# End of attention: the gate's operands of the first token block made in weight buffers at steps 116 to 119, and later loads moved behind the output weights

## The chip, the cores and the metric

The kernel runs on one NeuronCore of one Trainium2 chip. The metric is the time of one execution on the device in microseconds (us), median of several runs. Engine names are those of the profile: PE is TensorE, DVE is VectorE, ACT is ScalarE, POOL is GpSimd, SP is SyncE, the queue from which most DMA transfers are issued.

## What is computed

One layer of a hybrid encoder: a state-space branch and a chunked attention branch share one input projection; their outputs are normalised, concatenated and projected, and a SwiGLU feed-forward part follows. Sizes: 2048 tokens, model width 1024, 512 channels for each branch, 8 attention heads of 64, chunks of 64 frames with 8 chunks to the left, feed-forward width 2816, float32.

```python
def reference(x, ...):
    h = rmsnorm(x, norm_mix_g[l])
    proj = h @ w_in[l]
    y_ssm = s5_mixer(u_ssm, ...)            # ends: y = gelu(y); y = y * sigmoid(y @ w_glu + b_glu)
    y_att = chunked_attention(q, k, v, attn_rel_bias[l])
    mixed = concatenate([rmsnorm(y_ssm, norm_ssm_out_g[l]), rmsnorm(y_att, norm_att_out_g[l])])
    x = x + mixed @ w_out[l]
    h = rmsnorm(x, norm_ffn_g[l])
    x = x + (silu(h @ w_gate[l]) * (h @ w_up[l])) @ w_down[l]
    return rmsnorm(x, norm_final_g)
```

## The kernel before

Matmuls of high precision are made of three: an operand is split into a high half (a cast on ACT) and a low half (a subtraction on DVE); `split` (line 177) does this, and `mm3` (line 171) adds hi*hi, hi*lo and lo*hi in PSUM. Profile lines 81 and 84 are the wrappers through which all matmuls and transposes go.

**Attention** (`att_phase`, line 733) runs over 128 steps: 4 token blocks of 512, 4 head pairs, 2 heads, 4 query pieces. A step's scores `sc` come from PE; DVE adds the bias and finds the maximum (line 937), ACT takes the exponential (line 940), PE transposes (`pt`), and the transposed piece is split into `pth` (ACT, line 956) and `ptl` (DVE, line 957). After four pieces the products with `v` go to `pj`; `ya` (lines 981 and 990) is the attention output, which is stored to `ya_s` (line 991). Between these, generators called units bring in other work piece by piece: projections of later token blocks (their weights lie in three buffers `w` of [128, 2, 1024], line 753, last used for the last projections), the state-space branch, and from step 120 (`GSTART`) on the first `MIX_N` pieces of `mix_phase`.

Two helpers set the order: `behind()` (line 739) makes an instruction stand behind the last exponential in its engine's list (`k.least`), and `issue_after(k.low)` behind the last `ptl`. The lists are fixed when the program is built; each engine works its list in order, and SP's DMAs stand in one list too.

A pool `lp` lasts beyond attention and keeps the tags listed in `LASTING` (line 39), among them the split gate weights `Wg`, which are made at steps 90 to 102, and `raw`, two buffers of [128, 1024] that from step 107 hold the four tiles `ys` of block 0. The state-space output of blocks 0 and 1 is fetched at steps 107 to 110 (`y0`), goes through gelu on ACT at steps 109 to 117, and is copied into `ys` on POOL (line 1058).

**The mixing phase** (`mix_phase`, line 1088) takes the four token blocks in turn. For each block `take` provides `ys`, `load` splits the four tiles of `ys` into `gh0..3` and `gl0..3` of the phase's own pool `my`, and `glu` makes the gate: four groups f of 12 matmuls of 128x512 (four k-tiles by three), then sigmoid and multiply. For block 0 the gate is in attention's spare PSUM tiles `pf`, the biases are added on DVE into `yr` (line 1183), and one sigmoid and four multiplies (lines 1185, 1187) follow at the end. For block 1 the groups go to tiles `big`. `rstd1` sums squares over channels (`pf<-ones,sq`, a few narrow matmuls) and takes the reciprocal roots on DVE (`newton`, lines 110 to 118, the last of which is `k.last_root`), `spread` puts them over all partitions with four transposes, and `rstd2` (line 1204) multiplies `ya` or `ys` by them. `mixed` splits the results into `m0..m7`, and `w_out` multiplies by the split output weights `woh`, `wol`, adds to `xt` and stores. `split_wo` splits eight pieces of w_out: two loaded early into buffers `xt` of pool `wr`, four into tiles `m..` of pool `mx`, two more into the `xt` buffers again once these are split.

`fetch` (line 1131) loads `yr`, the raw state-space output of blocks 2 and 3, with four DMAs; it is called when block 2 is taken. Between blocks 1 and 3 `pre_steps` prepares the first feed-forward inputs in spare tiles that `pre_tiles` hands out. The seam, where PE goes from w_out to the feed-forward part, is at about 911 us.

At the end of attention the code is:

```python
b, nxt = take(0), take(1)
for f in range(4):
    with tc.issue_after(k.least):
        load(b, f)
    yield
...
for f in range(4):
    load(nxt, f)
yield
pb = bk()
spread(k, te, pb[:, :512], b.o[0], 0)
rstd2(b, 0, pb[:, :512])
for n, _ in enumerate(glu(nxt, bk)):
```

`bank()` gives a tile of attention's PSUM pool; `bk()` gives one of that pool or, once attention has handed PSUM over, a `big` tile of two banks.

Of the kernel before, what the change touches and what calls it, by code (L numbers as in the profile page):

```python
# [16 lines left out]
P = 128  # L17
# [20 lines left out]
GATES = 90, 94, 98, 102  # L38
LASTING = "hi0", "lo0", "hi1", "lo1", "hi2", "lo2", "xt", "raw"
R1 = 10  # L40
# [692 lines left out]
def att_phase(k, ident, S, aw, x0, roots):  # L733

    tc, nc, io, pfs = k.tc, k.nc, k.io, k.pfs
    with ExitStack() as cx:
# [303 lines left out]
        for s in range(N + LAG + 2):  # L1040
# [9 lines left out]
            for o in TURNED.get(s % 32, ORDER) if s < N - 32 else ORDER:  # L1050
# [12 lines left out]
                elif o == "f":  # L1063
# [9 lines left out]
                    if s in GATES:  # L1073
                        q = GATES.index(s)
                        tags = [("xt", XB)] * 2 if q == 3 else [(f"hi{q}", 1), (f"lo{q}", 1)]
                        k.Wg[q] = [k.t(k.lp, n, [P, DS], F32R, bufs=c) for n, c in tags]
                        with behind():
                            split(k, k.Wg[q][0][:], k.Wg[q][1][:], wg[q // 2][:, q % 2 * DS : q % 2 * DS + DS])
            if s in FETCHES:
                f = FETCHES.index(s)  # L1080
                nc.sync.dma_start(k.y0[:, f], S["y"][:, f * P : (f + 1) * P, :128].rearrange("j p t -> p j t"))
        yield mix


MIX_N = 21


def mix_phase(k, S, bank):
# [3 lines left out]
    with ExitStack() as cx:  # L1092
# [10 lines left out]
        def load_wo(n, pool, tag, **kw):  # L1103
            raw = k.t(pool, tag, [P, 1024], **kw)
            nc.sync.dma_start(raw[:], io["w_out"][QS[n] * P : (QS[n] + 1) * P, :])
            return raw

        def split_wo(raws):
            for n, q in enumerate(QS):
                W[q] = k.t(mx, f"woh{q}", [P, D], F32R), k.t(mx, f"wol{q}", [P, D], F32R)  # L1110
                raw = raws[n] if n < len(raws) else load_wo(n, wr, "xt")
                with tc.issue_after(k.last_root) if n > 1 else nullcontext():
                    split(k, W[q][0][:], W[q][1][:], raw[:])
# [17 lines left out]
        def fetch(sb):  # L1131
            yrs[0] = k.t(my, "yr", [P, 4, L, 128])
            for f in range(4):
                nc.sync.dma_start(yrs[0][:, f], S["y"][:, f * P : (f + 1) * P, sb * 64 : sb * 64 + 128].rearrange("j p t -> p j t"))  # L1134

        def take(sb):
# [6 lines left out]
            else:  # L1143
                yt = k.t(my, "ys", [P, 4, SB])
                b.ys = [yt[:, f] for f in range(4)]
            b.g = []
            if sb == 2:
# [21 lines left out]
        def glu(b, bank, late=False):  # L1169
# [5 lines left out]
            for f in range(4):  # L1175
                ps = bank()
                cs = slice(f * P, (f + 1) * P)
                for q in range(4):
                    mm3(te, ps[:, :512], Wg[q][0][:, cs], Wg[q][1][:, cs], b.g[q][0][:], b.g[q][1][:], q == 0, q == 3)
                    if q < 3:  # L1180
                        yield
# [77 lines left out]
        def pre_tiles():  # L1259
            while True:  # L1260
                for f in range(4):
                    for m in "hl":
                        yield k.t(my, f"g{m}{f}", [P, SB])
                t = k.t(my, "yr", [P, 4, L, 128])[:].rearrange("p a b c -> p (a b c)")
                for i in range(8):
                    yield t[:, i * SB : (i + 1) * SB]

        yrs[0] = k.t(my, "yr", [P, 4, L, 128])
        b, nxt = take(0), take(1)
        for f in range(4):  # L1270
            with tc.issue_after(k.least):
                load(b, f)
            yield
        g = glu(b, bank, True)
# [12 lines left out]
        for f in range(4):  # L1287
            load(nxt, f)
        yield

# [600 lines left out]
```

## Time and profile before

| | |
|---|---|
| median of 3 runs | 2211.99 us |
| lowest, highest | 2210.46, 2216.73 us |
| profiled execution, its own time | 2214.67 us |
| profiled execution, span | 2212.9 us |
| PE busy | 2155.7 us, 97% |
| DVE, ACT busy | 69%, 46% |
| mean granted clock of PE | 0.992 |

The span is measured by the profiler from the first to the last instruction. PE is busy nearly throughout, so the places that matter are those where it stands still or runs at a lower granted clock. The places of the change lie between 597 us (the first copy into `ys`) and 715 us; attention's last transposed piece is split at 674 us, and the first w_out matmul of block 0 starts at 693.73 us. A row of the timeline gives start, duration, engine, line, operation, output<-inputs (buffer numbers left out), shape, count, and in brackets the idle time before it and what ended it.

### The profile page before, as it was taken

To read this page: it belongs to the slowest core of one execution; us is meant where nothing else is said; L and a number is where in the kernel's file an instruction comes from. 1 tells how busy PE (TensorE), PEld (TensorE's weight loads), DVE (VectorE), ACT (ScalarE), POOL (GpSimd) and SP (SyncE) were. 2 spreads that over 40 slices of the span, in tenths; PEclk is the share of its full clock that TensorE was granted. 3 is DMA by queue.
4 is the path that set the end of the run, shared out by engine and by line. 5 is a ranking of instruction groups with operands and counts; after the bars stand their busy time and mean duration, and the time that the engine had idled before them with its cause. 6 is when DMAs were issued, how large, how long until landed. Compare 5 with 4: busy or idle time off the path is not lost.

```text
span 2212.9 us, 30057 instructions
## 1 busy us (share of the span) xinstructions
PE 2155.7 (97%) x10606; PEld 1816.1 (82%) x10606; DVE 1534.3 (69%) x2667; ACT 1008.1 (46%) x1684; POOL 371.5 (17%) x839
## 2 busy tenths in 40 slices
PE   8999999999998999999999999999999999999998
PEld 6787898998977888788888887888888788888887
DVE  8767566565568657767776768767665477689785
ACT  6356566555677521533333345333333443354332
POOL 3367777676110000000000000000000100000000
PEclk9999999999999999999999999999999999999999
DMA  9788977665633346835555657545332395465552
GB/s 323 240 284 268 303 229 241 210 202 174 202 111 138 119 143 218 262 100 182 177 174 190 211 189 262 194 159 203 110 113 102 123 390 179 164 220 197 193 216 77
DMA packets 194423, 431.20 MB, mean 195 GB/s; under 512 B 19744, under 2 KB 37200, under 8 KB 187168
## 3 DMA queue, kind: packets, MB, share of 16 engines
q1 hardware_dynamic: 186448, 404.05, 54.7%
q0 software_dynamic: 7824, 25.24, 3.8%
q8 instruction: 83, 1.36, 0.3%
q14 instruction: 68, 0.56, 0.1%
HBM read 290.00 MB, written 131.10 MB: 190 GB/s over the span
## 4 chain that ended last, share of the span: by engine, by line
PE 61%; DMA 5%; DVE 2%; ACT 1%; issue 1%; SPq 0%; DVEq 0%; ACTq 0%
PE X L81 21%; PE ps L81 17%; PE Y L81 11%; PE big L81 6%; PE W L81 5%; DMA acc<-x 2%; DMA lo<-hc 1%; DMA x<-xt 1%; DVE xt L1239 0%; DMA hd<-wc 0%; DMA m<-in_w_out 0%; ACT hi L179 0%; DMA hc<-gh 0%; DVE acc L1664 0%; SPq L1134 0%
## 5 line engine op out<-in xcount | busy, mean ns | idle before, releaser
L81 PE MATMUL X<-hi,c 128*128 128x512 f32 x1408 | 451.7, 392 | 9.6 <-DVE c L179 5.0
L81 PE MATMUL ps<-hd,hd 128*128 128x512 f32 (+1 forms) x1920 | 428.8, 384 | 3.4 <-DVE hd L179 2.0
L81 PEld LDWEIGHTS ps<-hd,hd 128*128 128x128 f32 x1920 | 353.3, 188 | 75.1 <-DVE hd L179 2.7
L81 PEld LDWEIGHTS X<-hi,c 128*128 128x128 f32 x1408 | 265.8, 189 | 66.5 <-DVE c L179 5.9
L81 PE MATMUL X<-lo,c 128*128 128x512 f32 x704 | 275.3, 391 | 0.0
L179 ACT CAST hd<-hd 128x1536 fp32r<-128x1536 f32 (+1 forms) x106 | 147.5, 1394 | 230.7 <-DMA hd<-hq 164.9
L81 PE MATMUL Y<-hi,c 128*128 128x512 f32 x704 | 224.8, 390 | 1.5 <-DVE u L1526 1.5
L179 DVE TENSOR_TENSOR hd<-hd 128x1536 fp32r<-128x1536 f32 (+1 forms) x106 | 174.2, 1645 | 35.9 <-ACT hd L179 35.1
L179 DVE TENSOR_TENSOR c<-S,c 128x512 fp32r<-128x512 f32 x176 | 120.9, 688 | 101.0 <-ACT c L179 100.8
L1630 POOL DMA_DIRECT2D hd<-hq x7 | 5.2, 745 | 1072.0 <-PE X L81 1060.7
L1522 ACT COPY u<-X 128x512 f32<-128x512 f32 x132 | 77.4, 587 | 197.7 <-PE X L81 197.7
L179 ACT CAST c<-S 128x512 fp32r<-128x512 f32 x176 | 109.4, 622 | 121.7 <-PE Y L81 62.0
L81 PE MATMUL big<-m,woh 128*128 128x512 f32 x512 | 161.2, 396 | 0.0
L81 PEld LDWEIGHTS Y<-hi,c 128*128 128x128 f32 x704 | 132.7, 189 | 29.9 <-DVE u L1526 2.2
L1664 DVE TENSOR_TENSOR acc<-acc,ps 128x512 f32<-128x512 f32 x196 | 130.3, 683 | 38.5 <-PE ps L81 38.0
L81 PEld LDWEIGHTS X<-lo,c 128*128 128x128 f32 x704 | 132.9, 189 | 27.5
L179 ACT CAST c<-raw 128x512 fp32r<-128x512 f32 x132 | 82.2, 623 | 148.8 <-PE Y L81 73.0
L81 PE MATMUL pf<-hi,w 128*128 128x512 f32 x416 | 148.8, 410 | 0.0
L81 PE MATMUL Y<-lo,c 128*128 128x512 f32 x352 | 137.2, 390 | 0.0
L957 DVE TENSOR_TENSOR ptl<-pt,pth 128x640 fp32r<-128x640 f32 (+3 forms) x152 | 98.3, 646 | 46.1 <-ACT pth L956 42.1
L940 ACT ACTIVATE s<-s,mn 128x640 f32<-128x640 f32 (+4 forms) x128 | 97.9, 765 | 51.4 <-DVE mn L937 50.9
L956 ACT CAST pth<-pt 128x640 fp32r<-128x640 f32 (+3 forms) x152 | 83.8, 551 | 81.2 <-PE pt L84 75.7
(494 smaller groups left out, 4281.3 us busy)
## 6 DMA issues: line engine op xcount, KB each, us to landing
w<-wss SPq DMA_DIRECT2D x36, 1024.0 KB, 6.1
hq<-g SPq DMA_DIRECT2D x140, 256.0 KB, 2.1
hd<-hq SPq DMA_DIRECT2D x35, 768.0 KB, 4.4
hd<-wc SPq DMA_DIRECT2D x35, 768.0 KB, 5.9
raw<-in_w_gate SPq DMA_DIRECT2D x44, 512.0 KB, 3.6
raw<-in_w_up SPq DMA_DIRECT2D x44, 512.0 KB, 4.1
wc<-px SPq DMA_DIRECT2D x66, 256.0 KB, 3.1
wss<-w SPq DMA_DIRECT2D x12, 1024.0 KB, 6.3
```

Source lines behind the costliest of these rows:

```text
L81: return self.tc.keep_in_program_order(self.tc.nc.tensor.matmul(*a, **b))
L179: return nc.scalar.copy(hi, raw), nc.vector.tensor_tensor(lo, raw, f32(hi), op=ALU.subtract)
L940: nc.scalar.activation(s[:, :nk], s[:, :nk], AF.Exp, bias=mn[:], scale=-1.0, accum_out=sums[sb, pr][:, hh, qp : qp + 1])
L956: nc.scalar.copy(pth[:, a:b, qp, :], pt[:, a:b, :])
L957: k.low = nc.vector.tensor_tensor(ptl[:, a:b, qp, :], pt[:, a:b, :], f32(pth[:, a:b, qp, :]), op=ALU.subtract).ins
L1522: nc.scalar.copy(u[:], ps[:])
L1630: (nc.gpsimd if aside else nc.sync).dma_start(f32(lo), src.rearrange("g p c -> p g c"))
L1664: V.tensor_tensor(a, a, ps[:], op=ALU.add)
```

## The change

- The tag `w` joins `LASTING`, so that the three weight buffers are kept until the feed-forward part.
- At step 116 two of them become `k.G`; at steps 116 to 119 (`HEADS`) one tile of block 0's `ys` each is split into a quarter of `k.G`, under `behind()`. The four pieces that did this in `mix_phase` go, and `MIX_N` is 17 instead of 21.
- All four blocks use `k.G` as gate operands (`gate_operand`); `gh*` and `gl*` go. `ys` of blocks 1 and 3 lies in the third `w` buffer. `pre_tiles` hands out pieces of `w` buffers in place of the `g` tiles.
- The `yr` loads are put behind the last load of w_out.
- Only splits of w_out from the fifth on stand behind the last reciprocal root, instead of from the third on.
- The `spread` of block 0's attention roots and the multiplies `rstd2` are written one piece earlier, with a tile of `bank()`.

```diff
-LASTING = "hi0", "lo0", "hi1", "lo1", "hi2", "lo2", "xt", "raw"
+LASTING = "hi0", "lo0", "hi1", "lo1", "hi2", "lo2", "xt", "raw", "w"
+HEADS = 116, 117, 118, 119
...
+            if s == HEADS[0]:
+                k.G = [k.t(k.lp, "w", [P, 2, 1024], F32R, bufs=WB) for _ in range(2)]
+            if s in HEADS:
+                f = HEADS.index(s)
+                with behind():
+                    split(k, *gate_operand(k, f), k.ys[f])
...
-MIX_N = 21
+MIX_N = 17
+def gate_operand(k, f):
+    fs = slice(f % 2 * SB, f % 2 * SB + SB)
+    return k.G[f // 2][:, 0, fs], k.G[f // 2][:, 1, fs]
...
-            nc.sync.dma_start(raw[:], io["w_out"][QS[n] * P : (QS[n] + 1) * P, :])
+            k.last_wo = nc.sync.dma_start(raw[:], io["w_out"][QS[n] * P : (QS[n] + 1) * P, :]).ins
...
-                with tc.issue_after(k.last_root) if n > 1 else nullcontext():
+                with tc.issue_after(k.last_root) if n > 3 else nullcontext():
...
-                nc.sync.dma_start(yrs[0][:, f], S["y"][...])
+                with tc.issue_after(k.last_wo):
+                    nc.sync.dma_start(yrs[0][:, f], S["y"][...])
...
-                yt = k.t(my, "ys", [P, 4, SB])
-                b.ys = [yt[:, f] for f in range(4)]
-            b.g = []
+                if sb == 1:
+                    k.y1 = k.t(k.lp, "w", [P, 4, SB], bufs=WB)
+                b.ys = [k.y1[:, f] for f in range(4)]
...
-            gh, gl = k.t(my, f"gh{f}", [P, SB], F32R), k.t(my, f"gl{f}", [P, SB], F32R)
-            split(k, gh[:], gl[:], b.ys[f])
-            b.g.append((gh, gl))
+            split(k, *gate_operand(k, f), b.ys[f])
...
-                for f in range(4):
-                    for m in "hl":
-                        yield k.t(my, f"g{m}{f}", [P, SB])
+                for _ in range(2):
+                    t = k.t(k.lp, "w", [P, 4, SB], bufs=WB)
+                    for i in range(4):
+                        yield t[:, i]
...
         b, nxt = take(0), take(1)
-        for f in range(4):
-            with tc.issue_after(k.least):
-                load(b, f)
-            yield
         g = glu(b, bank, True)
...
         for f in range(4):
             load(nxt, f)
+        pb = bank()
+        spread(k, te, pb, b.o[0], 0)
+        rstd2(b, 0, pb[:])
         yield
...
-        pb = bk()
-        spread(k, te, pb[:, :512], b.o[0], 0)
-        rstd2(b, 0, pb[:, :512])
```

Three places show what this does to the lists. The first is DVE in the last attention steps, before and now; `s,mn` is the bias and maximum of a step, `k` the last keys, `gl` and `w` the low halves of the gate's operands, made from `raw`.

```order
L857 TENSOR_TENSOR k_1693_7796<-pf_7852,k_1693_7796 64x512
L857 TENSOR_TENSOR k_1696_7799<-pf_7852,k_1696_7799 64x512
L179 TENSOR_TENSOR gl_1726_7979<-raw_7422,gh_1725_7978 128x512
L957 TENSOR_TENSOR ptl_7920<-pt_7952,pth_7919 128x5x128
L937 ISA s_7987,mn_7988<-sc_7982,nba_98 128x640
L937 ISA mn_7988 128x1
L967 RECIPROCAL rs_8044<-sm_7635 128x8
L957 TENSOR_TENSOR ptl_7920<-pt_7992,pth_7919 128x5x128
L179 TENSOR_TENSOR gl_1733_8001<-raw_7422,gh_1732_8000 128x512
L179 TENSOR_TENSOR gl_1735_8005<-raw_7423,gh_1734_8004 128x512
```

Now:

```order
L180 TENSOR_TENSOR w_7856<-raw_7422,w_7856 128x512
L958 TENSOR_TENSOR ptl_7745<-pt_7827,pth_7744 128x5x128
L938 ISA s_7867,mn_7868<-sc_7862,nbb_1553 128x640
L938 ISA mn_7868 128x1
L856 SCALAR_TENSOR_TENSOR q2l_7795<-pf_7802,q2h_7794 64x512
L856 SCALAR_TENSOR_TENSOR q2l_7798<-pf_7802,q2h_7797 64x512
L180 TENSOR_TENSOR w_7856<-raw_7422,w_7856 128x512
L958 TENSOR_TENSOR ptl_7745<-pt_7871,pth_7744 128x5x128
L938 ISA s_7900,mn_7901<-sc_7895,nbb_1553 128x640
L938 ISA mn_7901 128x1
L180 TENSOR_TENSOR w_7857<-raw_7423,w_7857 128x512
```

The first three subtractions now stand beside the last queries `q2l`, ahead of the last keys (`k`), and the fourth a few rows further on; before, all four stood behind the keys; the casts on ACT move in the same way.

The second is DVE from the last subtraction of block 1's operands to the `ya` multiplies (line 1204 before, 1216 now), before and now. `pf_8332` is a tile in attention's PSUM bank 1, `big_8392` one of the tiles after the hand-over.

```order
L179 TENSOR_TENSOR gl_1810_8343<-ys_7973,gh_1809_8342 128x512
L1187 TENSOR_TENSOR raw_7422<-raw_7422,yr_7972 128x512 x2
L1187 TENSOR_TENSOR raw_7423<-raw_7423,yr_7972 128x512 x2
L1123 TENSOR_TENSOR sq_8319<-sq_8319,sg_8321 128x512
L981 TENSOR_TENSOR ya_8203<-pj_8350,yt_8367 64x512
L1123 TENSOR_TENSOR sq_8319<-sq_8319,sg_8324 128x512
L990 TENSOR_TENSOR ya_8203<-ya_8203,pj_8370 128x512
L1123 TENSOR_TENSOR sq_8319<-sq_8319,sg_8327 128x512
L1204 SCALAR_TENSOR_TENSOR ya_1758_8115<-ya_1758_8115,ga_7967,big_8392 128x512
L1204 SCALAR_TENSOR_TENSOR ya_1759_8116<-ya_1759_8116,ga_7967,big_8392 128x512
```

Now:

```order
L180 TENSOR_TENSOR w_7857<-w_7981,w_7857 128x512 x2
L1216 SCALAR_TENSOR_TENSOR ya_1737_8042<-ya_1737_8042,ga_7975,pf_8332 128x512
L1199 TENSOR_TENSOR raw_7422<-raw_7422,yr_7980 128x512 x2
L1199 TENSOR_TENSOR raw_7423<-raw_7423,yr_7980 128x512 x2
L1136 TENSOR_TENSOR sq_8313<-sq_8313,sg_8315 128x512
L1216 SCALAR_TENSOR_TENSOR ya_1738_8043<-ya_1738_8043,ga_7975,pf_8332 128x512
L1136 TENSOR_TENSOR sq_8313<-sq_8313,sg_8318 128x512
L1216 SCALAR_TENSOR_TENSOR ya_1739_8044<-ya_1739_8044,ga_7975,pf_8332 128x512
L1136 TENSOR_TENSOR sq_8313<-sq_8313,sg_8321 128x512
L1216 SCALAR_TENSOR_TENSOR ya_1740_8045<-ya_1740_8045,ga_7975,pf_8332 128x512
L982 TENSOR_TENSOR ya_8226<-pj_8345,yt_8362 64x512
L991 TENSOR_TENSOR ya_8226<-ya_8226,pj_8365 128x512
```

The four multiplies moved ahead of the last two `ya` of attention and between the adds of squares. On PE the first gate group of block 1, `big_8387`, takes banks 0 and 1, and its first matmul waits for the last of these four multiplies; before, `big_8392` had banks 0 and 1, the first two groups had banks 6 and 7 and 4 and 5, and it was the second that waited, for line 990.

The third is SP's list behind the store of attention's next to last `ya_s`, before and now.

```order
L1134 DMA yr_8908<-y_65 128x8x128 x4
L1105 DMA m_1834_8499<-in_w_out 128x1024
L1105 DMA m_1835_8501<-in_w_out 128x1024
L1105 DMA m_1836_8503<-in_w_out 128x1024
L1105 DMA m_1837_8505<-in_w_out 128x1024
L1105 DMA xt_8545<-in_w_out 128x1024
L1105 DMA xt_8551<-in_w_out 128x1024
L1166 DMA ya_1911_8933<-ya_s_66 128x512
```

Now:

```order
L1118 DMA m_1820_8485<-in_w_out 128x1024
L1118 DMA m_1821_8487<-in_w_out 128x1024
L1118 DMA m_1822_8489<-in_w_out 128x1024
L1118 DMA m_1823_8491<-in_w_out 128x1024
L1118 DMA xt_8531<-in_w_out 128x1024
L1118 DMA xt_8537<-in_w_out 128x1024
L1148 DMA yr_8894<-y_65 128x8x128 x4
L1178 DMA ya_1889_8911<-ya_s_66 128x512
```

The four `yr` loads moved from ahead of the six loads of w_out to behind them.

More of the change, by code (lines that the diff above doesn't have):

```diff
@@ L1133, in fetch @@
             for f in range(4):
-                nc.sync.dma_start(yrs[0][:, f], S["y"][:, f * P : (f + 1) * P, sb * 64 : sb * 64 + 128].rearrange("j p t -> p j t"))
+                with tc.issue_after(k.last_wo):
+                    nc.sync.dma_start(yrs[0][:, f], S["y"][:, f * P : (f + 1) * P, sb * 64 : sb * 64 + 128].rearrange("j p t -> p j t"))
         def take(sb):
@@ L1178, in glu @@
                 for q in range(4):
-                    mm3(te, ps[:, :512], Wg[q][0][:, cs], Wg[q][1][:, cs], b.g[q][0][:], b.g[q][1][:], q == 0, q == 3)
+                    mm3(te, ps[:, :512], Wg[q][0][:, cs], Wg[q][1][:, cs], *gate_operand(k, q), q == 0, q == 3)
                     if q < 3:
```

## The prediction

> **What bounds the kernel now.** The first view read was the chain of waits over the whole program. TensorE holds most of it, so a stall anywhere else counts only where TensorE stands still for it.
>
> ```profile
> PE 61%; DMA 5%; DVE 2%; ACT 1%; issue 1%; SPq 0%; DVEq 0%; ACTq 0%
> ```
>
> The second view was the timeline of TensorE (start, duration, what, and in brackets its idle time before and the releaser), from the last attention steps to the output projection. Its idle places there, two rows without idle that mark where block 1's gate and w_out begin (677.76, 693.73), and the end of the mixing phase:
>
> ```profile
> 640.04 1.33 PE L84 MATMUL pt<-ident,s 128*128 128x128 f32 x5 [1.89 <-DVE ptl L957]
> 643.01 1.33 PE L84 MATMUL pt<-ident,s 128*128 128x128 f32 x5 [0.57 <-DVE ptl L957]
> 674.57 0.50 PE L81 MATMUL pj<-ptl,v 128*128 128x512 f32 x1 [0.36 <-DVE ptl L957]
> 677.76 0.48 PE L81 MATMUL big<-gh,hi 128*128 128x512 f32 x1
> 682.89 0.47 PE L81 MATMUL big<-gh,hi 128*128 128x512 f32 x1 [2.14 <-DVE ya L990]
> 693.73 0.62 PE L81 MATMUL big<-m,woh 128*128 128x512 f32 x2
> 698.49 0.50 PE L81 MATMUL big<-m,wol 128*128 128x512 f32 x1 [2.78 <-DVE wol L179]
> 699.62 0.50 PE L81 MATMUL big<-m,wol 128*128 128x512 f32 x1 [0.17 <-DVE wol L179]
> 914.64 0.47 PE L81 MATMUL X<-hi,c 128*128 128x512 f32 x1 [3.26 <-DVE xt L1239]
> 916.99 1.22 PE L81 MATMUL X<-hi,c 128*128 128x512 f32 x2 [1.64 <-DVE c L179]
> ```
>
> The last two rows are the seam, where the feed-forward part (X) follows the last output projection. The stalls at 698.49 and 699.62 hang on the split output weights. The third view, the chain of waits inside this stretch, says why those weights are late: SP, which issues the loads, issued the four yr loads (line 1134) late, and the loads of w_out (line 1105) only behind them.
>
> ```profile
> 680.25 0.37 SPq L1134
> 686.75 6.97 DMA m<-in_w_out
> 697.30 2.28 DVE wol L179 x2
> 699.62 8.69 PE big L81 x37
> ```
>
> The fourth view is the table by stage, columns: the stretch, its length, busy time and instructions of TensorE, its weight loads, VectorE, ScalarE and GpSimd, then the granted TensorE clock, the DMA share and GB/s.
>
> ```profile
> 616.00:620.00 4.00, 3.62 (x23) 3.07 (x22) 3.92 (x7) 2.54 (x6) 0.00 (x0) 1.00 0.26 70
> 628.00:632.00 4.00, 4.00 (x24) 3.54 (x23) 2.16 (x4) 3.77 (x5) 1.00 (x1) 1.00 0.53 114
> 640.00:644.00 4.00, 3.39 (x15) 2.99 (x15) 2.71 (x6) 2.85 (x6) 0.07 (x1) 0.50 0.68 215
> 644.00:648.00 4.00, 4.00 (x19) 3.57 (x18) 3.15 (x7) 3.04 (x6) 0.00 (x0) 0.72 1.02 394
> 684.00:688.00 4.00, 4.00 (x12) 3.16 (x11) 4.00 (x8) 3.82 (x6) 0.00 (x0) 0.60 1.12 350
> 696.00:700.00 4.00, 1.34 (x5) 0.82 (x6) 3.90 (x8) 4.00 (x6) 0.00 (x0) 1.00 0.89 345
> 916.00:920.00 4.00, 3.01 (x7) 2.44 (x8) 2.74 (x5) 1.58 (x3) 0.00 (x0) 0.50 1.01 263
> 920.00:924.00 4.00, 4.00 (x13) 3.10 (x13) 3.70 (x6) 3.47 (x7) 0.00 (x0) 0.66 0.87 339
> ```
>
> Three of the idle places cost more than their length, since the granted clock falls behind them. Busy time times what the clock lacks of 1 is the loss: behind 640.04 it is 3.39 x 0.50 + 4.00 x 0.28 = 2.8 us, behind 682.89 4.00 x 0.40 = 1.6, at the seam 3.01 x 0.50 + 4.00 x 0.34 = 2.9. Around the 2.78 us at 698.49 the clock stays at 1.00.
>
> **First term: splits at steps 116 to 119.** The operands of block 0 are now split before the last steps instead of during them. What they hold up now is this on VectorE and ScalarE:
>
> ```profile
> 636.58 0.62 ACT L179 CAST gh<-raw 128x512 fp32r<-128x512 f32 x1
> 638.64 1.66 ACT L179 CAST gh<-raw 128x512 fp32r<-128x512 f32 x3
> 638.29 0.84 DVE L179 TENSOR_TENSOR gl<-raw,gh 128x512 fp32r<-128x512 f32 x1
> 642.87 1.28 DVE L179 TENSOR_TENSOR gl<-raw,gh 128x512 fp32r<-128x512 f32 x2
> ```
>
> The cast of 636.58 and the subtraction of 638.29 stand ahead of the pth and ptl for which TensorE waits at 640.04; so do the ones after them at 643.01. Four casts and four subtractions leave that place. Of the 1.89 + 0.57 = 2.5 us of idle I keep about 0.6, since the chain of scores, exponential, transpose and ptl is itself close behind TensorE; 1.9 us go. With that much less idle the slow stretch of 2.8 us should not come; as the transposes and scores in it also wait on each other, I take 2.1 of it. The waits on ptl that follow up to 674.57, a few tenths each like its 0.36, give perhaps 0.6 more, because the gate's matmuls, started one to three pieces earlier in the list, lie better between the transposes. Attention's last ptl then ends **4.6 us** earlier. The price is cover: eight instructions of about 0.65 us move into 616 to 636, where TensorE is full and ScalarE's idle time in a window of 4 goes from 1.46 us (616 to 620) down to 0.23 (628 to 632). Replaying ScalarE's list with casts in these gaps puts no exponential more than 0.5 us late, and TensorE loses about 0.2 (in the 4.6). Without the cover the four casts cost 2.5 us of TensorE. Bounds of the term: 2.1, and with all of the idle and of the slow stretch gone 5.9.
>
> **Second term: a new wait in front of block 1's gate.** These rows carry it.
>
> ```profile
> 673.69 0.82 DVE L957 TENSOR_TENSOR ptl<-pt,pth 128x640 fp32r<-128x640 f32 x1 [1.51 <-ACT pth L956]
> 675.09 2.49 DVE L179 TENSOR_TENSOR gl<-ys,gh 128x512 fp32r<-128x512 f32 x4
> 677.61 2.50 DVE L1187 TENSOR_TENSOR raw<-raw,yr 128x512 f32<-128x512 f32 x4
> 680.02 0.68 DVE L1123 TENSOR_TENSOR sq<-sq,sg 128x512 f32<-128x512 f32 x1
> 683.26 2.72 DVE L1204 SCALAR_TENSOR_TENSOR ya<-ya,ga,big 128x512 f32<-128x512 f32 x4
> 675.66 1.92 ACT L1185 ACTIVATE yr<-yr 128x2048 f32<-128x2048 f32 x1
> 676.94 0.62 PE L84 MATMUL pj<-ident,rb 128*128 128x128 f32 x4
> ```
>
> Before, the spread of the attention's reciprocal roots went to a tile of its own, and the first two gate groups could start at 677.76 while VectorE multiplied; the 2.14 us came only at the second group. Now the spread lies in one of attention's PSUM banks, and the first gate group of block 1 is written to that bank. Its first matmul waits for the last of the four multiplies that read the spread, and behind it in TensorE's list stand all four gate groups and w_out. VectorE's list up to that multiply, from the last ptl, with 4.6 us taken off: ptl done at 674.43 - 4.6 = 669.8; four splits 2.5 (675.09 to 677.61), the first multiply 0.65 (a quarter of 2.72), four raw multiplies 2.4 (677.61 to 680.02), then three adds of 0.6 and three multiplies of 0.65 in turn, 3.8. That is 679.2. ScalarE's sigmoid ends at 677.58 - 4.6 = 673.0, just when the raw multiplies want it. TensorE is through with attention at 676.94 + 0.62 - 4.6 = 673.0 and so stands idle for **6.3 us**, against 2.14.
>
> The four groups took 693.73 - 677.76 = 15.97 us; less 2.14 of idle and less 1.6 for the slow stretch they need 12.2. From 679.3 that gives 691.5 at full clock. Full clock isn't to be had after 6.3 us of standing still: 1.6 were lost behind 2.14 us of idle, 2.9 at the seam behind 3.26 and 1.64. The new idle is nearer to the seam's, and I take 2.4 between these bounds: 693.9.
>
> [...]
>
> **Third term: w_out's loads ahead of the yr loads.** SP's list is in order.
>
> ```profile
> 653.09 0.32 SPq L991 DMA_DIRECT2D ya_s<-ya  x1
> 680.25 4.76 SPq L1134 DMA_DIRECT2D yr<-y  x4
> 685.06 3.32 SPq L1105 DMA_DIRECT2D m<-in_w_out  x4
> 690.23 1.43 SPq L1105 DMA_DIRECT2D xt<-in_w_out  x2
> yr<-y SPq DMA_DIRECT2D x4, 512.0 KB, 6.5
> ```
>
> Between 653.09 and 680.25 it only waits. The four m loads can now go right behind 653.09, and with 3.32 us to issue and 6.97 to land are in place by some 663. The low halves of the third and fourth weight no longer wait for the reciprocal roots either. So the stalls of 2.78 and 0.17 go: **2.95 us**. The two xt loads still wait for the splits of the two weights whose buffers they take, about 687; the four yr loads follow by 693 and land 6.5 us later (the last row: size and time from issue to landing) at some 699, against 691 before. Their first reader is the gelu after the second half of the mixed operands, at 713.47 before:
>
> ```profile
> 713.47 4.20 ACT L1155 ACTIVATE raw<-yr 128x512 f32<-128x512 f32 x4
> ```
>
> That leaves over 10 us. The ya loads behind them slip by up to 2 us; without their slack ScalarE would hold the mixed operands by as much. I cost both at nothing, with 2 as the bound.
>
> **The sum.** w_out began at 693.73 and lost 2.95: as if at 696.7. Now it begins at 693.9 without a stall: 2.8 us earlier. In parts: 4.6 from attention and 2.95 from the weights, less 4.2 of longer idle (6.3 - 2.14) and 0.8 of more slow clock, which is 2.55; the rest is the 0.2 us between 677.56 and 677.76 in which TensorE made the spread, and which now lies earlier. From there to the seam TensorE runs without a break over a few tenths, so the gain is carried. The seam's own waits, 3.26 and 1.64, are chains behind TensorE's last matmuls and move along; that the third preparation tile is free only some 7 us later I cost at nothing, as by my count its reader is over 10 us behind. The profiled execution, with a span of 2212.9 and a time of 2214.67, becomes 2211.9; it lies 2.7 above the median of the three runs, 2211.99, to which the same gain gives **2209.2 us**.
>
> **Rivals.**
>
> *ScalarE loses the early steps (slower).* The casts and subtractions go in at a place where in-order queues have 0.23 to 1.46 us to spare in each 4. If the exponentials are late by the whole 2.5 us, TensorE idles between 616 and 636, and a slow stretch of 1.6 to 2.9 comes there in place of the one at 640. Then attention ends when it did or up to a microsecond later, block 1's gate begins at 683.9 to 684.9, and w_out at 698.5 to 699.5 against 696.7: slower by 2 to 3, 2214 to 2215; with the ya loads' 2 us and two slow stretches more further on, up to 2222. It decides from the point where the first term falls under 1.8. For it: ScalarE's 3.77 of 4 at 628 to 632. Against it: TensorE's 4.00 of 4 in the same row, with ScalarE as full.
>
> *The wait on the bank is cheap (faster).* If attention's own end comes another 2 us earlier or VectorE gets to the multiplies sooner (by taking them ahead of the raw multiplies, 2.4), w_out begins at 689 to 691, and VectorE's wol splits hold it next: 6 to 8 us gained, 2204 to 2206, by the median. Against it: the order on VectorE is fixed as shown.
>
> *The change doesn't pay at all.* The weights come early but VectorE, still solid from the last ptl on, delivers wol no sooner: the 2.95 stays, and the sum is 2212. VectorE's list has two wol splits and the m splits ahead, which end near 690 by my count, against 698.4; so I hold it for unlikely.
>
> *A late seam.* The third preparation tile slips by its whole landing time, 6.5 us: 2216. For it: the seam's waits of 3.26 and 1.64 show a chain without slack there. Against it: the slack of over 10 us above.
>
> **How the numbers follow.** Forecast 0.48, with a range of its own of 2205 to 2213; ScalarE's loss 0.28; cheap wait 0.13; no pay 0.05; late seam 0.06. A measurement of this kernel tells about 0.3%, 6.6 us, from no change: 2205.4 and 2218.6 are the bounds. Beyond the lower lie the cheap wait and a fifth of the forecast (the first term at 5.9 together with the shorter slow stretch), 0.23; beyond the upper half of ScalarE's loss, two thirds of the late seam (where it meets a smaller first term) and 0.04 for what no case has, 0.22; the rest, 0.55, is no change. The range is 2203 to 2218.
>
> **What would show it.** Right: in the changed profile no idle over 0.7 us on TensorE between 616 and 650 and full clock at 640 to 648; the last attention transpose about 4 to 5 us earlier; one idle of 6 to 7 us ahead of the first big matmul, released by VectorE's ya multiply, and a clock near 0.5 behind it; m loads issued near 653; no wait on wol. Wrong: idle at 616 to 636, the last ptl where it was, a wait on yr or ya on ScalarE after 700, or longer idle at the seam than 3.3 and 1.6.

## The result and the profile after

| | before | after |
|---|---|---|
| median, first session (13 runs each) | 2216.73 us | 2208.76 us |
| lowest, highest | 2210.37, 2219.57 | 2205.53, 2213.99 |
| ratio to before, 95% interval | | 0.9970, 0.9962 to 0.9978 |
| median, second session (20 and 11 runs) | 2214.80 us | 2209.55 us |
| ratio to before, 95% interval | | 0.9973, 0.9964 to 0.9982 |
| span of the profiled execution | 2212.9 us | 2207.0 us |

The change makes the kernel faster by 0.30% (0.22 to 0.38, 4.9 to 8.4 us), and by 0.27% (4.0 to 8.0 us) in the second session. The predicted 2209.2 us is met almost exactly, but partly by luck: the three runs from which it was worked out (2211.99) lay low. The forecast gain was 2.8 us, and 5.3 and 8.0 were measured between the medians of the two sessions. The case to which the prediction gave most, no change beyond 0.3% (0.55), came out at its very edge: with 13 runs on each side the gain is small, but clear of the noise.

The timeline of TensorE in the changed kernel, at the places shown of before (start, duration, what, and in brackets its idle time before and the releaser):

```profile
638.22 0.77 PE L85 MATMUL pt<-ident,s 128*128 128x128 f32 x5 [1.02 <-DVE ptl L958]
678.63 1.19 PE L82 MATMUL big<-w,hi 128*128 128x512 f32 x2 [6.35 <-DVE ya L1216]
723.46 1.05 PE L82 MATMUL big<-ones,sq 128*128 128x1 f32 x8 [1.38 <-DVE nv L111]
911.62 0.73 PE L82 MATMUL X<-hi,c 128*128 128x512 f32 x2 [3.22 <-DVE c L180]
915.05 0.74 PE L82 MATMUL Y<-hi,c 128*128 128x512 f32 x2 [0.42 <-DVE c L180]
```

The two stalls at 640 and 643 (1.89 and 0.57) have become one of 1.02. The 6.35 us ahead of block 1's gate are new. No stall on `wol` is left; in exchange 1.38 us come later, on the reciprocal root `nv`. At the seam the wait on `xt` is gone and that on the split weights `c` is longer.

The stages of the changed kernel (columns as in the prediction: stretch, length, TensorE, its weight loads, VectorE, ScalarE, GpSimd, granted clock, DMA share, GB/s):

```profile
616.00:636.00 20.00, 19.52 (x110) 16.71 (x109) 12.81 (x24) 18.50 (x29) 3.76 (x4) 1.00 0.26 68
616.00:620.00 4.00, 3.62 (x20) 2.90 (x19) 3.00 (x6) 3.58 (x7) 0.00 (x0) 1.00 0.45 122
628.00:632.00 4.00, 4.00 (x27) 3.69 (x27) 2.53 (x5) 3.94 (x5) 1.10 (x1) 1.00 0.29 65
640.00:644.00 4.00, 4.00 (x25) 3.45 (x23) 3.03 (x6) 3.88 (x8) 0.00 (x0) 1.00 0.99 320
644.00:648.00 4.00, 4.00 (x29) 3.76 (x28) 3.67 (x8) 3.46 (x6) 0.00 (x0) 1.00 1.01 389
676.00:680.00 4.00, 1.37 (x3) 1.16 (x4) 3.87 (x7) 2.23 (x4) 0.00 (x0) 0.50 0.01 2
680.00:684.00 4.00, 4.00 (x11) 3.08 (x10) 2.40 (x4) 0.00 (x0) 0.59 (x1) 0.50 0.19 70
684.00:688.00 4.00, 4.00 (x18) 3.21 (x17) 2.87 (x3) 3.77 (x6) 0.00 (x0) 0.90 0.00 0
916.00:920.00 4.00, 4.00 (x20) 3.26 (x19) 3.62 (x7) 1.91 (x3) 0.00 (x0) 1.00 0.95 315
```

ScalarE fills up to 3.94 of 4 at 628 to 632, and TensorE still has 4.00 of 4; over 616 to 636 it is busy for 19.52 of 20 us, against 19.62 by the same view of before. The cover for the moved splits holds. The clock at 640 to 648, which was 0.50 and 0.72, is 1.00. It is 0.50 from 676 to 684 instead, behind the new wait.

VectorE's list behind the last `ptl` gives the reason for the 6.35 us, and SP's list shows the reordered loads:

```profile
668.40 0.82 DVE L958 TENSOR_TENSOR ptl<-pt,pth 128x640 fp32r<-128x640 f32 x1 [0.92 <-ACT pth L957]
669.14 2.49 DVE L180 TENSOR_TENSOR w<-w,w 128x512 fp32r<-128x512 f32 x4
671.55 0.74 DVE L1216 SCALAR_TENSOR_TENSOR ya<-ya,ga,pf 128x512 f32<-128x512 f32 x1
672.21 2.49 DVE L1199 TENSOR_TENSOR raw<-raw,yr 128x512 f32<-128x512 f32 x4
677.74 0.74 DVE L1216 SCALAR_TENSOR_TENSOR ya<-ya,ga,pf 128x512 f32<-128x512 f32 x1
```

```profile
650.30 1.88 SPq L1118 DMA_DIRECT2D m<-in_w_out  x4
688.59 7.27 SPq L1148 DMA_DIRECT2D yr<-y  x4
695.90 2.00 SPq L1178 DMA_DIRECT2D ya<-ya_s  x2
701.91 0.94 SPq L1178 DMA_DIRECT2D ya<-ya_s  x2
```

The last of the four multiplies that read the bank ends at 677.74 + 0.74 = 678.48, and TensorE starts at 678.63. The m loads go out at 650.30, 35 us earlier than before; the yr loads go out at 688.59, and the ya loads behind them slip, from 691.71 before to 695.90 and 701.91.

### The profile page after: what moved, and what is told of

Same layout as the page of the kernel before. It is cut to its first block, busy times and chain, and to the rows that moved or that the text cites. A ratio compares the mean times of both kernels' runs of the same rounds, so it can differ in the third digit from the quotient of the medians.

```text
span 2207.0 us, 30050 instructions
## 1 busy us (share of the span) xinstructions
PE 2150.1 (97%) x10606; PEld 1813.1 (82%) x10606; DVE 1533.3 (69%) x2667; ACT 1005.0 (46%) x1682; POOL 371.2 (17%) x839
## 3 DMA queue, kind: packets, MB, share of 16 engines
q8 instruction: 83, 1.36, 0.3%
## 4 chain that ended last, share of the span: by engine, by line
PE 81%; DMA 5%; DVE 4%; POOL 4%; issue 3%; ACT 3%; SPq 0%; DVEq 0%; ACTq 0%; POOLq 0%
PE X L82 21%; PE ps L82 19%; PE Y L82 10%; PE big L82 9%; PE pf L82 9%; PE W L82 5%; PE pj L82 4%; PE pt L85 2%; PE sc L82 2%; DMA acc<-x 2%; POOL X L645 1%; POOL X L644 1%; POOL st L642 1%; POOL st L643 1%; POOL X L654 1%
```

## How the profiles are compared

One profiled execution differs from the next of the same kernel by up to 4 us, in good part because the places at which the clock drops differ (of the 4.0 us between the two of heads and loads, 2205.11 and 2201.10, the slow loss below makes up 2.2). So for each kernel TensorE's idle time between its matmuls was added up by stage (from the timeline, all gaps, also those too small for a bracket). Two executions are given where there are two. "Gate" is the length from the last `ptl` to the first w_out matmul; "w_out" is from there to 16 matmuls ahead of X; "seam" is from there to 100 matmuls behind the first of X. The slow loss is half of the busy time in stretches at half clock, over the whole program. The rows from coarse down are experiments that follow.

| us | start of last ptl | gate | idle in w_out | idle at seam | slow loss |
|---|---|---|---|---|---|
| before | 673.7, 676.0 | 20.0, 20.0 | 4.3, 3.4 | 4.9, 4.6 | 15.3, 13.9 |
| after | 668.4, 670.8 | 25.1, 24.2 | 1.9, 1.6 | 3.9, 2.4 | 11.3, 17.0 |
| coarse (of before) | 675.6 | 20.5 | 3.5 | 3.5 | 20.5 |
| heads alone | 668.7 | 17.7 | 4.8 | 2.3 | 16.2 |
| heads and loads | 670.5, 669.5 | 17.7, 17.7 | 2.9, 2.8 | 2.2, 3.3 | 11.6, 9.4 |
| spread back | 668.8 | 17.7 | 2.9 | 4.2 | 13.4 |
| loads back | 668.7 | 23.8 | 0.8 | 3.6 | 14.6 |
| copy of the spread | 671.1 | 18.2 | 4.8 | 4.4 | 14.7 |
| spread and loads back | 670.6 | 17.8 | 4.2 | 3.9 | 11.2 |
| condition back | 668.2, 671.1 | 24.4, 24.2 | 0.8, 0.8 | 3.1, 3.4 | 7.2, 9.6 |

## The experiments

The edits are against the changed kernel, but for coarse and the repeat of before. Ratios are to before, run on the same chip.

**The spread back behind the hand-over.** `spread` and the multiplies go where they stood, so the wait on the bank goes.

```diff
-        pb = bank()
-        spread(k, te, pb, b.o[0], 0)
-        rstd2(b, 0, pb[:])
         yield
...
+        pb = bk()
+        spread(k, te, pb[:, :512], b.o[0], 0)
+        rstd2(b, 0, pb[:, :512])
```

> The changed kernel with the spread of block 0's attention roots put back behind the PSUM hand-over (a big tile of its own), everything else of the change kept. Theory A (the new wait in front of block 1's gate is a true loss of some 4 us of idle and part of a slow stretch): the 6.35 us idle ahead of the first big matmul goes, an idle of 1 to 2 us ahead of the second gate group takes its place, w_out begins near 688 where it began at 693.5, and the time is 4 to 6 us below the changed kernel, ratio to before about 0.9945. Rival B (VectorE's list up to m and wol bounds w_out anyway, so the wait is only cover): idle of 4 us or more moves to w_out's first matmuls, time within 1.5 us of the changed kernel, ratio about 0.997.

Measured: 2206.65 us, 0.9962 (0.9950 to 0.9973). TensorE's long waits in it:

```profile
677.33 0.70 PE L82 MATMUL big<-w,hi 128*128 128x512 f32 x2 [1.46 <-DVE ya L991]
717.70 1.86 PE L82 MATMUL big<-ones,sq 128*128 128x1 f32 x8 [2.42 <-DVE nv L111]
```

The gate's 25 us become 17.7, and no wait on `wol` comes in. But 2.42 us of it are given back at 717.70, where the chain of the ya loads, gelu, mixed operands and roots is not earlier. The time is about 2 us below the change, not the 4 to 6 that were expected. By itself this is not clear of the noise: the interval of the change holds 0.9962.

**The yr loads ahead of w_out's again.**

```diff
-                with tc.issue_after(k.last_wo):
+                if True:
```

> The changed kernel with the four yr loads back ahead of the loads of w_out on SP, everything else kept. My prediction on record (the order on SP is worth the 2.95 us of stall): a wait on wol of 2 to 3 us returns in w_out, time 2 to 3 us above the changed kernel, ratio about 0.998 to 0.9985. Theory C (with attention's end 4.6 us earlier and w_out held by the new wait, the weights come in time even behind the yr loads): m loads issue near 679 and land by 688, no wait on wol over 0.5 us, time as the changed kernel, ratio about 0.997.

Measured: 2208.77 us, 0.9969 (0.9958 to 0.9980), the same as the change.

```profile
678.89 1.19 PE L82 MATMUL big<-w,hi 128*128 128x512 f32 x2 [6.34 <-DVE ya L1216]
721.37 1.05 PE L82 MATMUL big<-ones,sq 128*128 128x1 f32 x8 [0.26 <-DVE nv L111]
```

The 6.34 us stand, no stall on `wol` returns, and the 1.38 on `nv` falls to 0.26. With the gate held and the condition changed, the order of the loads is worth nothing.

**The heads alone**: the splits at steps 116 to 119 and the kept buffers; the spread, the loads and the condition on the last root as before.

```diff
-                with tc.issue_after(k.last_root) if n > 3 else nullcontext():
+                with tc.issue_after(k.last_root) if n > 1 else nullcontext():
```

(and the two edits above)

> Only the splits at steps 116 to 119 in the kept weight buffers, with their consequences for the tiles of later blocks; spread, yr loads and the splits of w_out as before the change. Theory A: attention's last ptl is as early as in the changed kernel (about 669), no 6.35 us idle; a stall on wol of 1 to 4 us stays in w_out; time 1 to 4 us below the changed kernel, ratio about 0.9955. Rival D (the gain needs the loads and the splits of w_out to come earlier): ratio 0.998 to 1.0, the stall on wol grows by what attention won.

Measured: 2209.90 us, 0.9974 (0.9963 to 0.9984).

```profile
677.26 0.70 PE L82 MATMUL big<-w,hi 128*128 128x512 f32 x2 [1.45 <-DVE ya L991]
692.50 0.80 PE L82 MATMUL big<-m,wol 128*128 128x512 f32 x1 [4.06 <-DVE wol L180]
```

The heads by themselves give as much as the whole change, although the stall on `wol` has grown from 2.78 to 4.06. The expected 0.9955 was missed, and so was the rival's 0.998 to 1.0.

**A copy of the spread.** ScalarE copies the spread from PSUM to SBUF, and the multiplies read the copy, so the bank is free after the copy.

```diff
-        rstd2(b, 0, pb[:])
+        pc = k.t(mz, "pc", [P, SB])
+        with tc.high_priority():
+            nc.scalar.copy(pc[:], pb[:])
+        rstd2(b, 0, pc[:])
```

> The changed kernel with the spread copied by ScalarE from its PSUM bank to SBUF right behind it, so that the first gate group waits only for that copy (one ScalarE copy of about 0.6 us more) and the four multiplies read SBUF. Theory A: idle of 6.35 us goes, an idle of 1 to 2 us comes ahead of the third gate group (it waits for the last ya of attention), time 4 to 6 us below the changed kernel, ratio about 0.9945. Rival B: as the changed kernel, 0.997.

Measured: 2207.53 us, 0.9966 (0.9954 to 0.9979).

```profile
682.88 0.69 PE L82 MATMUL big<-w,hi 128*128 128x512 f32 x2 [2.39 <-DVE ya L991]
708.46 0.51 PE L82 MATMUL big<-m,woh 128*128 128x512 f32 x1 [0.78 <-ACT m L180]
722.84 1.56 PE L82 MATMUL big<-ones,sq 128*128 128x1 f32 x8 [3.24 <-DVE nv L111]
```

The first gate group no longer waits, so it was the bank that held it. w_out starts 18.2 us behind the last `ptl` instead of 24 to 25, and half of that comes back: idle time in w_out rises from 1.9 and 1.6 us to 4.8 (0.78 and 3.24 of it in the rows above; the 2.39 is ahead of the third gate group, on the last `ya`). The time can't be told from that of the change; 4 to 6 us less were expected.

**Coarse tiles in before.** The operands `gh`, `gl` of before lie in two tiles of four, as the change's `w` buffers do, and nothing else is changed. This gives SP's list at the seam the order that it has in the change: the feed-forward inputs of the second cycle are loaded behind the store of the first.

```diff
-            gh, gl = k.t(my, f"gh{f}", [P, SB], F32R), k.t(my, f"gl{f}", [P, SB], F32R)
-            split(k, gh[:], gl[:], b.ys[f])
+            if f % 2 == 0:
+                b.t = k.t(my, f"g{f}", [P, 4, SB], F32R)
+            gh, gl = (b.t[:, 2 * (f % 2) + m] for m in range(2))
+            split(k, gh, gl, b.ys[f])
```

> The kernel before with one edit: gh and gl of two tiles of ys each share one tile of [128, 4, 512], and the tiles that the feed-forward preparation gets in blocks 2 and 3 are quarters of these, as in the changed kernel; SP's list from 765 to 912 us is then that of the changed kernel (three x loads stand behind a store of x1 that they stood ahead of). Theory S (part of the gain comes from the seam, where the last input load was late behind that list): attention and w_out as before, but the wait on xt of 3.26 us at the seam goes to under 1, time 2 to 5 us below before, ratio about 0.9985. Rival (the seam gained only because everything came earlier or by the draw of the clock's windows): seam waits of 3 and 1.6 us as before, ratio 1.000.

Measured: 2213.92 us, 0.9993 (0.9981 to 1.0005).

```profile
915.92 0.47 PE L81 MATMUL X<-hi,c 128*128 128x512 f32 x1 [1.36 <-DVE xt L1241]
918.28 1.22 PE L81 MATMUL X<-hi,c 128*128 128x512 f32 x2 [1.65 <-DVE c L179]
```

The wait on `xt` is 1.36 instead of 3.26; that on `c` stays. All idle time at the seam is 3.5 us, against 4.9 and 4.6 in before and 2.2 to 4.4 in everything that has the heads. So the new tiles shorten the seam, by some 1.3 us in this one profile; 0.07% of 2215 is 1.5, which the runs alone can't tell from nothing. The chain of waits points the same way, but not in every profile. In both profiles of before it reaches the seam over SP and the loads of the preparations; the rows are of the first:

```profile
876.38 5.62 DMA hc<-gh
884.90 0.38 SPq L1468
909.03 4.12 DMA xt<-in_xt
```

With the coarse tiles it runs over TensorE's own last w_out matmuls instead, and so it does in the first profile of the change, whose rows follow. In the second it goes over the loads again, though no wait on `xt` is left there either.

```profile
886.15 21.80 PE big L82 x96
907.96 1.14 DVE xt L1251
```

**Spread and loads as before, condition changed**: the first and the second edit together.

> Experiment e1 (spread behind the hand-over) with the yr loads ahead of the w_out loads too. Theory C (the order on SP matters only where block 1's gate is not held by the new wait): w_out begins near 686.5 as in e1, the weights land near 688, a stall on wol of 2 to 4 us comes, time 2 to 3 us above e1, ratio about 0.9975. Rival (the stall only moves a wait that comes later anyway, as the 2.42 us ahead of 717 in e1): stall comes, but w_out of block 0 ends no later against e1 than 1 us, ratio 0.9962 to 0.9967.

Measured: 2206.45 us, 0.9957 (0.9941 to 0.9973).

```profile
690.98 0.50 PE L82 MATMUL big<-m,wol 128*128 128x512 f32 x1 [0.52 <-DVE wol L180]
721.73 1.06 PE L82 MATMUL big<-ones,sq 128*128 128x1 f32 x8 [2.17 <-DVE nv L111]
```

With the condition changed, and with the loads in the old order, the stall on `wol` is 0.52 where the heads alone have 4.06. So the condition alone takes away nearly all of it; the expected stall of 2 to 4 us didn't come. The chain of waits in before shows why. The weights land at 693.72 (the `m<-in_w_out` row of the prediction), but the split `wol` begins only at 697.30. Between them stand a sigmoid on ScalarE, the multiply `ys` that waits for it, and the last steps of the root:

```profile
695.33 0.59 ACT sg L1190
695.94 0.69 DVE ys L1191
697.13 0.16 DVE no L118
```

**The condition on the last root back** (`n > 1`), everything else as changed; run twice.

> The changed kernel with the third and fourth split of w_out put back behind the last reciprocal root. On VectorE the roots ended at 694.3, w_out wants the third low half at 694.9: a wait on wol of 0.5 to 2 us, time 0 to 1.5 us above the changed kernel, ratio 0.997 to 0.9977. Rival (this condition alone made the stall of 2.78): a wait of 2.8 us, ratio 0.9983.

> The change with the splits of the third and fourth output weight behind the last reciprocal root again, a second time. Theory: the condition is idle here, since TensorE is held by the wait on the bank until 678.5 and the weights are in time with or without it; then the ratio is that of the change beside it within 0.001, and the 0.9954 of the first try was a draw. Rival: the splits behind the root leave ScalarE and VectorE free for something that counts later; then it is again lower by 0.0015 or more.

Measured: 2205.14 us, 0.9954 (0.9939 to 0.9969), then 2209.71, 0.9976 (0.9966 to 0.9986), beside 0.9973 for the change. TensorE waits 6.35 us in front of the gate in both, never on `wol`, and on `nv` for 0.25 and 0.26 instead of 1.38 and 1.09 in the two profiles of the change. The second try doesn't confirm the first, and none of these waits tells the two profiles apart, so I take the first for a draw; that it was one isn't shown. It is also a warning: two tries of one kernel differed by 0.22%, with intervals that hardly touch.

**Before once more**, with a profile.

> The kernel before once more, for its trace: which idle places come back with the same length, and where the slow stretches of the clock lie this time. Theory W (a window of 3.41 us that is idle for over half makes the next one slow, and the windows lie differently in each execution): idle of 1.9, 2.1, 2.8 and 3.3 us at the same places to 0.2 us, slow stretches at other ones of them; waits at the seam within 0.5 us of 3.26 and 1.64.

Measured: 2215.64 us, one run; its numbers are the second ones in the table. The stalls at 640, ahead of the gate, on `wol` and at the seam are in both executions of before, so they belong to the kernel. The slow stretches behind the stalls at 640, ahead of the gate and at the seam came in both too, against the expectation that they would lie at others of these places. Others did not repeat: those at 728 and 783 us were in the first only (half clock from 728.17 and from 782.79, each for 3.41 us); in the second two matmuls of w_out take 0.61 to 0.63 us there, as at full clock.

**The change once more, and the best of the parts.** The last kernel has the heads and the new order of loads, with the spread and the condition as before (the first edit and `n > 1`).

> The change once more, unaltered, beside the two versions that follow. If its gain is that of the heads and of a shorter seam, its ratio comes out at 0.997 again, within 0.996 to 0.998. If the 0.997 was largely a draw of the clock's windows, it lies above 0.998.

> The spread of the attention's roots behind the hand-over again and the condition on the reciprocal root back, so of the change the heads and the order of SP's loads are left. Theory (the wait on the bank costs little, since what is won ahead of w_out is given back at the chain of ya loads, gelu and mixed operands, and at the seam): within 0.0015 of the change beside it, w_out from about 686.5 with a wait on wol of up to 4 us. Rival (the wait of 6.35 us costs its length): lower than the change by 0.002 or more, 2204 us where that has 2208.

> Heads and the order of SP's loads alone once more. If the wait of 6.35 us on the bank costs a few us in the end (rival of the run before), the ratio is again 0.996 or lower. If it costs nothing that can be seen (theory), and the 0.9951 of the first try was a draw, it is 0.9965 to 0.9975, that of the change.

Measured: the change 0.9973, as in the table at the top; heads and loads 2204.03 us, 0.9951 (0.9936 to 0.9965), and on another chip 2202.79, 0.9952 (0.9939 to 0.9966).

```profile
678.06 0.70 PE L82 MATMUL big<-w,hi 128*128 128x512 f32 x2 [1.44 <-DVE ya L991]
691.19 0.50 PE L82 MATMUL big<-m,wol 128*128 128x512 f32 x1 [1.92 <-DVE wol L180]
718.84 1.05 PE L82 MATMUL big<-ones,sq 128*128 128x1 f32 x8 [0.25 <-DVE nv L111]
900.70 0.47 PE L82 MATMUL X<-hi,c 128*128 128x512 f32 x1 [0.60 <-DVE xt L1251]
```

This version beats both kernels: about 10.8 us less than before, and 0.18 to 0.22% (4.0 to 4.9 us) less than the change. Of the 6.6 us that go from the gate (24.3 to 17.7), 1.92 come back as a stall on `wol`. Here the number of the rival came, and the expectation that the wait is nearly free fell. But the comparison with the change holds two edits, the spread and the condition. What the wait alone costs is read from three pairs that differ in nothing else: the change (0.9970, 0.9973) against the spread put back (0.9962); both with the old order of loads, 0.9969 against 0.9957; both with the old condition, 0.9954 and 0.9976 against 0.9951 and 0.9952. In the means these are 0.10, 0.12 and 0.14%. None of the pairs is clear of the noise alone, but all point the same way: the wait costs some 2 to 3 us, less than half of the 6.6 that it adds at the gate.

## Why the prediction was right, and where it was not

**First term, 4.6 us: right, a little small.** From the first of the stalls to the last `ptl` the change takes 668.40 - 638.22 = 30.2 us, before took 673.69 - 640.04 = 33.7, and the stall itself shrinks by 0.9: 4.3. Over all profiles the last `ptl` comes at 675.1 in the mean of three profiles without the heads, and at 669.7 in eleven with them: 5.4. The idle time from the start to there fell by 2.1 and the slow loss by 3.2; a slow stretch of 6.83 us at 640 is in all three without the heads and in none of the eleven with them. The prediction kept back 0.7 of the 2.8 us of the slow stretch because "the transposes and scores in it also wait on each other"; in the profile the stretch is gone as a whole. ScalarE's loss, the likeliest rival at 0.28, didn't come: 616 to 636 costs TensorE 0.10 us more than before (19.62 less 19.52), and in the change's second profile nothing. Of the prediction's own signs one was missed here: no idle over 0.7 us was to come between 616 and 650, and 1.02 did. Two slips in its working change nothing: 1.9, 2.1 and 0.6 make 4.6 without the 0.2 us of loss that is said to be in it, and the last `ptl` ended at 674.51, not at 674.43.

**Second term: right in place, cause and size.** 6.3 us forecast, 6.35 found, released by the multiply named; 2.4 us of slow clock forecast, and 1.37 x 0.5 + 4.00 x 0.5 + 4.00 x 0.1 = 3.1 found. For the shorter slow stretch in the forecast's chances no run had a figure beforehand; the change lost the 3.1, and in the kernel with the loads back a matmul behind the same wait takes 0.63 us instead of 0.39 from 678.89 to about 682.4, by estimate a loss of 3.5 x 0.5 = 1.8. w_out was forecast at 693.9 and starts at 693.47. The kernel with the copy shows that it is the bank, and not VectorE's load as such, that holds the gate. The rival of the cheap wait has the time that heads and loads reach (2204 to 2206 was its forecast), but by another way: the wait was not cheap in the change, it had to be taken out.

**Third term, 2.95 us: right in size, wrong in its cause.** The prediction put the end of the stalls down to the loads ahead of the yr loads first, and to the condition beside them. It read the lateness of the weights off SP alone; the rows of the chain that it left out, from 693.72 to 697.30, hold the root. Without the wait heads alone stall for 4.06 us, with the loads 1.92, with the condition changed 0.52, with both (the spread put back) not at all. With the gate held, one of the two was undone at a time, and no stall came back. Both undone with the wait kept was not run. But in the kernel with heads alone the late weight is there 23.8 us behind the last `ptl` (692.50 less 668.75), and with the wait w_out only begins 23.8 to 25.1 us behind it: by this estimate the delay that costs 4.3 us at the gate would have hidden the stall by itself. The bound of 2 us for the ya loads was touched, which the prediction had named as a sign of being wrong: 0.81 us on ScalarE at 707.86, 1.38 on TensorE at 723.46. They need both edits: with the loads undone the first is gone and the second is 0.26, with the condition undone likewise (0.25 and 0.26).

```profile
707.86 0.63 ACT L1135 ACTIVATE sg<-ya 128x512 f32<-128x512 f32 x1 [0.81 <-DMA ya<-ya_s]
```

**The step that failed: "The seam's own waits, 3.26 and 1.64, are chains behind TensorE's last matmuls and move along".** The wait on `xt` doesn't. In before the `xt` of the seam was loaded by SP behind the loads of other preparations, as the chain above shows, and the order and time of these changed with the new tiles. Idle time at the seam went from 4.9 and 4.6 us to 3.9 and 2.4. The late seam was a rival; the opposite happened. The coarse tiles show the tile's part in it.

**The sum with measured terms**, with the two profiles of before against the five that have the wait on the bank: 5.4 from attention (as above), less 4.3 at the gate (20.0 to 24.3), and 2.7 of idle time in w_out (3.83 to 1.16) and 1.5 at the seam (4.8 to 3.3) make 5.3 us, against 2.8 forecast and 5.3 to 8.0 between the medians. Later idle time is 1.2 us lower in the mean, for which no cause is shown. The clock's draws stay open: the slow loss of the change is 11.3 us in one execution and 17.0 in another, which covers before's 15.3 and 13.9, so no gain may be put down to it beyond the stretch at 640.

## What to carry to other kernels

Take a bundle of edits apart before keeping it: here one part gave 0.26% alone, one cost some 2 to 3 us, and of two others each looked idle while that wait and the other one were there. When an operand is moved to a PSUM tile that is free earlier, look up who gets that bank next and how long the readers of the operand are queued: here the first matmul in the bank waited 6.35 us for the last of them, with everything behind it. A stall that vanishes because its reader has been delayed isn't a gain; ask whether it comes back when the delay is removed.

## What the runs showed of the hardware

In the first profiles of before and of the change the granted clock is 1.00 or 0.50. Each slow stretch lasts 3.41, 6.83 or 10.24 us, but for the one that the end of the program cuts off, and within a profile they all begin a whole number of times 3.41 us apart (at 499.48, 639.43, 683.80 and 915.91 in before, at 500.46, 674.54 and 725.74 in the change, among others). Cut into windows of that length, some stages around slow stretches read so (columns as above), first before, then the change:

```profile
636.02:639.43 3.41, 1.59 (x9) 0.82 (x7) 3.29 (x6) 3.36 (x7) 3.41 (x4) 1.00 0.29 72
639.43:642.85 3.42, 2.40 (x9) 2.00 (x9) 2.13 (x5) 2.31 (x6) 0.64 (x1) 0.50 0.50 160
642.85:646.26 3.41, 3.25 (x12) 2.96 (x13) 3.21 (x7) 2.99 (x7) 0.00 (x0) 0.50 1.02 366
680.39:683.81 3.42, 1.28 (x6) 0.82 (x5) 3.36 (x6) 0.63 (x1) 0.59 (x1) 1.00 0.52 140
694.04:697.46 3.42, 1.67 (x8) 1.05 (x6) 1.42 (x6) 3.42 (x5) 0.00 (x0) 1.00 1.02 413
697.46:700.87 3.41, 2.21 (x8) 1.53 (x9) 3.41 (x5) 3.41 (x6) 0.00 (x0) 1.00 0.62 239
```

```profile
671.13:674.54 3.41, 1.15 (x10) 0.91 (x8) 3.41 (x6) 2.67 (x5) 0.00 (x0) 1.00 0.00 0
674.54:677.96 3.42, 0.00 (x0) 0.00 (x0) 3.42 (x7) 2.49 (x5) 0.00 (x0) 0.50 0.01 2
681.37:684.78 3.41, 3.41 (x10) 2.63 (x9) 1.02 (x2) 0.61 (x2) 0.00 (x0) 0.50 0.22 82
684.78:688.20 3.42, 3.42 (x16) 2.80 (x15) 3.07 (x4) 3.36 (x6) 0.00 (x0) 1.00 0.21 17
```

A window in which TensorE is busy for 1.28 of 3.42 us (0.63 idle) or for 1.59 of 3.41 (0.53 idle) has a slow one behind it; one with 1.67 of 3.42 (0.51 idle) has not. That fits the two stalls: the 2.14 us at 682.89 lay in one window, and a slow one with 3.41 us of busy time came behind it, a loss of 1.7 us; the 2.78 us at 698.49 were shared between two (0.51 and 0.35 idle) and cost no clock. Counted over these two profiles from 20 us on, a full-speed window idle for 0.53 or more has a slow one behind it in 8 of 8 cases, one idle for 0.51 or 0.52 in 1 of 4 (behind 496.07 in before; not behind 694.04 there, nor behind 1350.38 and 1759.98 in the change), and one idle for less in 4 of 1248, each of these four with eight or sixteen matmuls of 128x1 in it. A slow window is followed by another in 5 of 5 cases where it is idle for 0.20 or more, and by full speed in 13 of 13 where it is idle for 0.18 or less; the stretch at 640 is two windows long, with 2.40 of 3.42 us busy in its first and 3.25 of 3.41 in its second. The windows lie otherwise in the two profiles (683.80 less 674.54 is 2.71 times 3.41), and a stall at the same place had a slow stretch behind it in one execution and none in another: the wait on `c` at the seam, 3.22 us in the first profile of the change, lay in two windows (0.49 and 0.46 idle) and had none, and in the second, 2.28 us long, it had one, in which a matmul takes 0.60 to 0.63 us from 914.19 to 917.16 and 0.39 to 0.42 from 917.59 on. The four slow windows behind narrow matmuls are at 725.74 in the change, after the eight of 128x1 at 723.46 and 1.38 us of idle, with 0.33 of the window idle; at 780.35 there, behind a window that is only 0.08 idle but holds sixteen of them; and at 728.17 and 782.79 in before, behind windows of 0.08 and 0.07 idle with sixteen each. 27 other full-speed windows that hold some had none behind them.
